# A two-block transformer kernel: the context's first modulation, norm and projections taken one k-tile at a time

## The chip, the cores and the metric

The kernel runs on one core of a Trainium2 chip. The metric is the device time of one execution in microseconds (us). Before the change three runs took 3097.56 to 3098.76 us, median 3098.48 us; one further execution was recorded by the hardware profiler, and every row below is from that one.

## The reference, cut to what matters

Two transformer blocks follow each other. The first has two layers and two streams: a latent stream of 512 tokens and a context stream of 256 tokens, both 1024 wide. Each layer starts with a modulated norm and one wide projection of each stream:

```python
mod = (jax.nn.silu(c) @ w_mod[l] + b_mod[l])[:, None, :]
mod_c = jax.nn.silu(c_ctx) @ w_mod[l] + b_mod[l]
sh1, sc1, ga1, sh2, sc2, ga2 = jnp.split(mod, 6, axis=-1)
sh1c, sc1c, ga1c, sh2c, sc2c, ga2c = jnp.split(mod_c, 6, axis=-1)
h = modulate(rmsnorm(x, g_norm1[l]), sh1, sc1)
hc = modulate(rmsnorm(xc, g_norm1[l]), sh1c, sc1c)
pf, mq, mk, mv, mo, mg, cq, ckv, kr = split_proj(h @ w_in[l])
pfc, mqc, mkc, mvc, moc, mgc, cqc, ckvc, krc = split_proj(hc @ w_in[l])
...
def modulate(h, shift, scale):
    return h * (1 + scale) + shift
```

So before the first projection of the context can run, its shift and scale (two of the six parts of `silu(c_ctx) @ w_mod[0]`) and its norm must be there. The rest of the program (Fourier mixing, an mLSTM, attention, MLPs, and the second block) is the same before and after.

## The kernel before

The feature dimension is cut into eight k-tiles of 128. A product in full precision is made of three passes over weights and activations that are split into a high and a low part: `gemm` (lines 194 to 196) issues `wh` times high, `wh` times low and `wl` times high for each k-tile. A weight unit comes through `wunit` (lines 158 to 177): a DMA on the SP queue into `wr`, a cast on ACT to `wh` (line 169), a subtraction on DVE to `wl` (line 170), in rings of three. A scheduler orders the instructions of each engine by priorities that the program sets; each engine then runs its own list strictly in that order.

The start of the program, layer 0:

- `mod_cols` makes `cs`, the two conditioning vectors through silu, as a column of two for each k-tile.
- `mod_first` makes the shift and scale of both streams. For each of four groups of 512 columns it loads eight weight tiles of 256 KB from `wmn` (SP queue), multiplies each with the two columns of `cs` (line 476, result 2x512), copies the row out on ACT (line 479), turns it by four transposes (line 483) and adds the bias on DVE (line 487). The two groups of the scale come first, then the two of the shift.
- `rms_bcast` (lines 251 to 274) makes one over the root mean square of each token: sums on TensorE (line 251), a power on POOL (line 222), a broadcast on TensorE (line 270), a copy on ACT (line 274, the tile `rb`).
- `mod_start` makes `cb`, the conditioning vectors on all partitions, for the modulations that DVE makes later (`mod_units`, line 442, done beside other work through a side queue): four broadcast DMAs of `cc`, then DVE and ACT work (lines 418 to 421).
- `norm_split` makes the normed, modulated activations of the context, each k-tile as high and low part: a multiply on DVE (line 285), a cast with bias on ACT (line 289), a subtraction on DVE (line 290).
- `in_tok` (lines 543 to 545) makes the token-major projections in 48 matmuls, 128x432 each; `in_qk` makes six feature-major units of 24 matmuls, 128x256 each, and their convolutions on DVE (lines 580 and 586).
- Then the latent stream's norm (same lines, 512 wide), and units that both streams share (24 matmuls of 256 columns for the context, 24 of 512 for the latents). The mLSTM gates of the context are added on DVE (line 642) and transposed on TensorE (lines 645 and 671).

The order of work around the change is thus: all of shift and scale, then the whole norm, then all products of `in_tok`, then the six units of `in_qk`.

## Time and profile before

| | before |
|---|---|
| median of 3 runs | 3098.48 us (3097.56 to 3098.76) |
| the profiled execution | 3100.99 us |
| its span on the core | 3099.2 us |
| TensorE (PE) busy | 3005.6 us, 97% of the span |
| VectorE (DVE) busy | 1869.3 us, 60% |
| ScalarE (ACT) busy | 1182.9 us, 38% |
| GpSimd (POOL) busy | 116.7 us, 4% |
| mean DMA rate over the span | 118 GB/s |
| mean granted TensorE clock | 0.984 |

The span is the time between the first and the last instruction of the core; the execution's own time lies 1.8 us above it. A clock of 1.00 is full speed (2.4 GHz), 0.50 the lower level (1.2 GHz). Times in the rows below count from the span's start.

### The profile page before, as it was taken

Reading aid. Unit: us, or ns where it says so; the run is one execution under the profiler, and the core shown is the slowest. Engines: PE = TensorE matmul, PEld = TensorE weight load, DVE = VectorE, ACT = ScalarE, POOL = GpSimd, SP = SyncE. Lnnn points to the kernel's source line nnn. Section 1 sums busy time; section 2 is a strip of 40 time slices with the busy share of each in tenths; the row PEclk is TensorE's granted clock in tenths of the full one; section 3 lists DMA queues with packets and bytes.
Section 4 is the critical chain, followed back from the end, with each engine's and each line's share of the span. In section 5 each row is a group of like instructions: output and inputs, shape, how many; then the busy total and the mean of one; then the engine's idle time right before and its main releaser. Section 6 shows DMA issues by size and latency. Waiting matters only on the chain.

```text
span 3099.2 us, 44553 instructions
## 1 busy us (share of the span) xinstructions
PE 3005.6 (97%) x17374; PEld 2557.9 (83%) x17374; DVE 1869.3 (60%) x3755; ACT 1182.9 (38%) x2101; POOL 116.7 (4%) x296
## 2 busy tenths in 40 slices
PE   8998899999999999999999999999999999999998
PEld 4788879788888877778888888999999878888886
DVE  5887756777655766543444666655555566655544
ACT  4455554353333455433334442322222442322223
POOL 1000000000000010000000100000000110000000
PEclk9999999999999999999999999999999999999999
DMA  8654535754555432122222312322222212322221
GB/s 307 200 181 143 152 94 180 240 177 161 170 169 168 141 119 84 38 82 96 95 95 91 109 42 76 100 84 94 89 89 92 100 49 76 109 92 96 95 95 68
DMA packets 138129, 367.14 MB, mean 118 GB/s; under 512 B 14864, under 2 KB 42960, under 8 KB 137920
## 3 DMA queue, kind: packets, MB, share of 16 engines
q1 hardware_dynamic: 135760, 361.59, 36.0%
q8 instruction: 137, 2.24, 0.3%
q10 hardware_dynamic: 1728, 2.24, 0.2%
q14 instruction: 72, 0.59, 0.1%
q0 software_dynamic: 432, 0.48, 0.1%
HBM read 349.09 MB, written 15.06 MB: 117 GB/s over the span
## 4 chain that ended last, share of the span: by engine, by line
PE 43%; issue 12%; DVE 1%; POOL 0%; ACT 0%; POOLq 0%; DVEq 0%; ACTq 0%
PE S L194 11%; PE S L196 11%; PE S L195 11%; PE D L1616 1%; PE S L1547 1%; PE S L1549 1%; PE S L1548 1%; PE S L1702 1%; PE D L1717 1%; PE S L1641 1%; PE S L1662 1%; PE D L1622 0%; PE S L1658 0%; PE D L1715 0%; PE D L1547 0%
## 5 line engine op out<-in xcount | busy, mean ns | idle before, releaser
L194 PE MATMUL S<-A,wh 128*128 128x512 f32 (+2 forms) x4416 | 1498.0, 340 | 12.8 <-ACT A L289 4.0
L196 PE MATMUL S<-A,wl 128*128 128x512 f32 (+2 forms) x4416 | 1492.4, 338 | 5.6 <-DVE wl L170 5.6
L195 PE MATMUL S<-A,wh 128*128 128x512 f32 (+2 forms) x4416 | 1493.2, 338 | 1.5 <-DVE A L185 1.4
L169 ACT CAST wh<-wr 128x1024 fp32r<-128x1024 f32 (+1 forms) x474 | 495.2, 1045 | 1380.0 <-PE S L195 862.0
L194 PEld LDWEIGHTS S<-A,wh 128*128 128x128 f32 x4416 | 835.7, 189 | 111.2 <-issue 6.1
L196 PEld LDWEIGHTS S<-A,wl 128*128 128x128 f32 x4416 | 835.8, 189 | 98.6 <-DVE wl L170 8.9
L195 PEld LDWEIGHTS S<-A,wh 128*128 128x128 f32 x4416 | 835.2, 189 | 94.9 <-DVE A L185 2.7
L170 DVE TENSOR_TENSOR wl<-wr,wh 128x1024 fp32r<-128x1024 f32 (+1 forms) x474 | 576.7, 1217 | 318.3 <-ACT wh L169 303.4
L442 DVE SCALAR_TENSOR_TENSOR wr<-wr,B 128x512 f32<-128x512 f32 x224 | 149.1, 686 | 73.1 <-DMA wr<-wmod 72.4
L212 DVE SCALAR_TENSOR_TENSOR A<-S,mod,A 128x512 f32<-128x512 f32 x144 | 107.7, 749 | 115.8 <-PE S L196 115.5
L210 DVE TENSOR_TENSOR A<-A,S 128x264 f32<-128x264 f32 (+1 forms) x168 | 85.3, 514 | 122.4 <-PE S L196 122.1
L185 DVE TENSOR_TENSOR A<-A,A 128x512 fp32r<-128x512 f32 (+3 forms) x168 | 102.3, 616 | 33.1 <-ACT A L184 32.8
L1869 DVE TENSOR_TENSOR A<-S,A 128x264 f32<-128x264 f32 (+1 forms) x66 | 34.3, 519 | 127.1 <-PE S L196 124.2
L184 ACT CAST A<-A 128x512 fp32r<-128x512 f32 (+3 forms) x168 | 93.1, 560 | 25.2 <-DVE A L1834 16.8
L1877 DVE SCALAR_TENSOR_TENSOR A<-A,S 128x264 f32<-128x264 f32 (+1 forms) x66 | 34.0, 515 | 86.7 <-PE S L196 84.4
L1024 PEld LDWEIGHTS S<-B,B 128*128 128x128 f32 x416 | 53.5, 194 | 16.5 <-issue 5.5
L1024 PE MATMUL S<-B,B 128*128 128x96 f32 x416 | 55.3, 276 | 4.5 <-ACT A L1029 2.3
L222 POOL TENSOR_TENSOR rnr<-rnv,mhalf 128x4 f32<-128x4 f32 (+1 forms) x19 | 23.5, 1238 | 951.7 <-DVE rnv L221 946.4
L580 DVE SCALAR_TENSOR_TENSOR A<-A,cw,A 128x512 f32<-128x512 f32 (+1 forms) x84 | 53.3, 635 | 2.6 <-ACT A L578 1.0
L996 PE MATMUL D<-A,A 96*128 96x256 f32 (+1 forms) x144 | 54.4, 482 | 0.0
L1079 ACT ACTIVATE A<-A 128x512 f32<-128x512 f32 x80 | 50.6, 632 | 2.2
L229 ACT ACTIVATE A<-A 128x512 f32<-128x512 f32 (+1 forms) x66 | 33.5, 535 | 45.8 <-DVE A L212 34.2
(410 smaller groups left out, 2872.2 us busy)
## 6 DMA issues: line engine op xcount, KB each, us to landing
wr<-wmod SPq DMA_DIRECT2D x112, 512.0 KB, 3.9
wr<-wup SPq DMA_DIRECT2D x96, 512.0 KB, 3.3
wr<-wdn SPq DMA_DIRECT2D x96, 512.0 KB, 3.5
wr<-win SPq DMA_DIRECT2D x78, 512.0 KB, 3.6
wr<-wg SPq DMA_DIRECT2D x44, 512.0 KB, 3.5
wr<-wu SPq DMA_DIRECT2D x44, 512.0 KB, 3.4
wr<-wd SPq DMA_DIRECT2D x44, 512.0 KB, 3.3
wr<-wout SPq DMA_DIRECT2D x40, 512.0 KB, 3.4
```

The lines of the kernel that those rows point to most:

```text
L169: nc.scalar.copy(hi, raw)
L170: nc.vector.tensor_sub(lo, raw, hi.bitcast(F32))
L184: self.nc.scalar.copy(hi, src)
L185: self.nc.vector.tensor_sub(lo, src, hi.bitcast(F32))
L194: nc.tensor.matmul(o, wh[:, k_w[i]], xh[:, ts], start=(i == 0), stop=False)
L195: nc.tensor.matmul(o, wh[:, k_w[i]], xl[:, ts], start=False, stop=False)
L196: nc.tensor.matmul(o, wl[:, k_w[i]], xh[:, ts], start=False, stop=(i == nk - 1))
L210: nc.vector.tensor_add(x[:, ts], x[:, ts], ps)
L212: nc.vector.scalar_tensor_tensor(out=x[:, ts], in0=ps, scalar=ga, in1=x[:, ts], op0=ALU.mult, op1=ALU.add)
L442: nc.vector.scalar_tensor_tensor(out=wf if i == len(which) - 1 else self.junk, in0=wf, scalar=1.0, in1=self.cb[s * 2 + hf], op0=ALU.mult, ...
L996: nc.tensor.matmul(sc[:, off : off + nk], qT[h][:, ts], kT[h], start=True, stop=True)
L1024: nc.tensor.matmul(yp, pT[:, kt], V[j][:, h * MD : h * MD + MD], start=(kt == 0), stop=(kt == tot // P - 1))
```

## The change

The modulations of shift and scale, the norm and most of the first products of the context now go k-tile by k-tile, in a new function `ctx_start`. For each of the eight k-tiles:

- four DMAs of 256 KB from `wmk` bring the 256 columns (scale and shift of this k-tile) of all eight input tiles;
- eight matmuls, each with 32 stationary columns of `cs` (two real, thirty zero) and 256 moving columns, write to one of four groups of 32 PSUM partitions, so that four partial sums stand under each other;
- ACT copies the 128x256 result out; two matmuls with the constant `sel` add the four groups and turn the result at once; DVE adds the biases (both streams) and makes the gain;
- `norm_split` runs for this k-tile alone;
- twelve matmuls of 128x256 add this k-tile's share to four of the six `in_qk` units (weights `wqk`, 256 KB a k-tile), and after every second k-tile twelve matmuls of 128x432 add to the `in_tok` results.

After the loop the four results are copied out, and `in_qk` has two units left. `mod_start` now makes `cb` by sixteen broadcast matmuls 128x128 and four ACT copies, with no DMA and no tanh of its own, and stands ahead of `rms_bcast`. The slots for modulation weights fall from 20 to 16.

```diff
@@ mod_start
+                ps = self.S.new([P, 512])
+                for k in range(4):
+                    nc.tensor.matmul(
+                        ps[:, k * P : k * P + P], self.cs[:, hf * 4 + k, s : s + 1].broadcast_to([P, P]), self.ident,
+                        start=True, stop=True,
+                    )
                 t = self.B.new([P, 512])
-                nc.sync.dma_start(out=t, in_=self.a["cc"][s, hf].partition_broadcast(P))
-                nc.vector.tensor_scalar_mul(t, t, 0.5)
-                nc.scalar.activation(self.junk, t, AF.Tanh)
-                nc.vector.scalar_tensor_tensor(out=t, in0=self.junk, scalar=1.0, in1=t, op0=ALU.add, op1=ALU.mult)
+                nc.scalar.copy(t, ps)
...
@@ mod_cols
+        wide = self.sm([P, KT, 32], "cs", bufs=1)
+        nc.gpsimd.memset(wide, 0.0)
...
+        nc.vector.scalar_tensor_tensor(out=wide[:, :, 0:2], in0=th, scalar=1.0, in1=cs, op0=ALU.add, op1=ALU.mult)
+        self.cs = wide
+        self.sel = self.sm([P, 2], "sel", bufs=1)
+        nc.scalar.dma_start(out=self.sel, in_=self.a["sel"])
+
+    def ctx_start(self, mr, nr, tr, xc, rb, mods, gn, hc):
...
+        sc, sh = part(mods[1], 1), part(mods[1], 0)
+        qk = [self.S.new([P, NX]) for _ in range(4)]
+        dm = self.pd.new([P, 2, 512])
+        dt = self.pd.new([P, 2, 512])
+        for k in range(KT):
+            ps = dm[:, 0, k % 2 * 256 : k % 2 * 256 + 256]
+            for q in range(KT):
+                if q % 2 == 0:
+                    w = mr.new([P, 2, 256])
+                    nc.sync.dma_start(out=w, in_=self.a["wmk"][k, q // 2])
+                g = q % 4 * 32
+                nc.tensor.matmul(ps[g : g + 32], self.cs[:, q], w[:, q % 2], start=(q < 4), stop=(q >= 4))
+                if q % 2:
+                    mr.drop(w)
+            row = nr.new([P, 256])
+            nc.scalar.copy(row, ps)
+            dd = dm[:, 1, k * 4 : k * 4 + 4].rearrange("p (i s) -> p i s", i=2)
+            for i in range(2):
+                nc.tensor.matmul(dd[:, i], row[:, i * P : i * P + P], self.sel, start=True, stop=True)
+            nr.drop(row)
+            cols = slice(k, k + KT + 1, KT)
+            for s in (1, 0):
+                nc.vector.tensor_add(mods[s][:, cols], dd[:, :, s], self.bmod[:, 0, cols])
+            kk = slice(k, k + 1)
+            nc.vector.scalar_tensor_tensor(
+                out=Ac[:, kk], in0=sc[:, kk], scalar=1.0, in1=gn[:, 0, 0, kk], op0=ALU.add, op1=ALU.mult
+            )
+            self.norm_split(nr, rb, hc, xc, NX, Ac, sh, [k])
+            hh, hl = hc[k]
+            wh, wl = self.wunit(self.a["wqk"][k])
+            for j, o in enumerate(qk):
+                cs = slice(j * P, j * P + P)
+                nc.tensor.matmul(o, wh[:, cs], hh, start=(k == 0), stop=False)
+                nc.tensor.matmul(o, wh[:, cs], hl, start=False, stop=False)
+                nc.tensor.matmul(o, wl[:, cs], hh, start=False, stop=(k == KT - 1))
+            if k % 2:
+                self.tok_products([dt[:, 0, 0:432], dt[:, 1, 0:432]], 0, hc, k // 2)
...
@@ the layer loop
+                else:
+                    steps, convs, qkc = self.in_qk(tr, pg, l, hc, NX, range(6), raws)
+                    call(steps[4:])
```

The order of TensorE's instructions, first place: the program's start, where the context's first product stands. In these rows `cs` is the conditioning tile, `A` names SBUF work tiles, `S` and `D` PSUM tiles, and the last entry is the shape of the result. Before:

```order
L476 MATMUL D_27_117<-A_35_139,cs_23_102 2x512
L251 MATMUL S_46_173<-ones_70,A_38_151 128x1
...
L270 MATMUL S_50_183<-ident_69,rnr_49_180 128x128
L476 MATMUL D_51_187<-A_52_188,cs_23_102 2x512
...
L476 MATMUL D_73_255<-A_81_277,cs_23_102 2x512
L543 MATMUL S_107_353<-wh_110_356,A_91_313 128x432
```

And now:

```order
L491 MATMUL D_64_199<-A_69_213,cs_23_102 32x256 x2
L415 MATMUL S_30_122<-ident_69,cs_23_102 128x128 x4
...
L247 MATMUL S_46_172<-ones_70,A_38_150 128x1
...
L498 MATMUL D_64_199<-sel_26_110,A_70_217 128x2 x2
L266 MATMUL S_50_182<-ident_69,rnr_49_179 128x128 x2
L491 MATMUL D_64_199<-A_75_246,cs_23_102 32x256 x2
...
L498 MATMUL D_64_199<-sel_26_110,A_79_262 128x2 x2
L512 MATMUL S_60_195<-A_51_186,wh_73_229 128x256
```

Before, all 32 column products (line 476) stand ahead of the first product of the context (line 543). Now those of two k-tiles do, and the sixteen broadcasts (line 415) stand ahead of the sums of the norm (line 247, line 251 of before).

Second place: TensorE where the latents' norm is made (rms sums, then broadcast, then the first shared units, where `wh_219` of before and `wh_233` of the change are the same weights). Before:

```order
L251 MATMUL S_191_720<-ones_70,A_190_718 128x1
L194 MATMUL S_223_805<-A_91_313,wh_219_795 128x256
L270 MATMUL S_195_734<-ident_69,rnr_194_731 128x128 x4
L195 MATMUL S_223_805<-A_91_313,wh_219_795 128x256
...
L194 MATMUL S_224_832<-A_167_682,wh_219_795 128x512
L194 MATMUL S_232_883<-A_91_313,wh_228_870 128x256
...
L645 MATMUL S_341_1706<-ident_69,A_340_1700 36x128
```

And now:

```order
L247 MATMUL S_205_803<-ones_70,A_204_801 128x1
L266 MATMUL S_209_817<-ident_69,rnr_208_814 128x128 x4
L190 MATMUL S_237_888<-A_51_186,wh_233_878 128x256
L191 MATMUL S_237_888<-A_51_186,wh_233_878 128x256
L190 MATMUL S_238_915<-A_181_765,wh_233_878 128x512
L191 MATMUL S_238_915<-A_182_766,wh_233_878 128x512
L695 MATMUL S_355_1789<-ident_69,A_354_1783 36x128
L721 MATMUL S_361_1808<-ident_69,A_354_1783 36x128
```

Before, two context units and most of a latent unit (70 matmuls) stand between the broadcast and the first gate transpose (line 645). Now four matmuls do (line 695 is line 645 of before), and the other 44 of the first shared unit come behind the transposes.

Third place: DVE from that norm's start to the gates' last addition. Before:

```order
L170 TENSOR_TENSOR wl_220_796<-wr_218_794,wh_219_795 128x1024
L442 SCALAR_TENSOR_TENSOR wr_222_801,macc_221_800<-wr_222_801,B_87_300 128x512
L221 TENSOR_SCALAR rnv_193_730<-S_191_720 128x4
L442 SCALAR_TENSOR_TENSOR wr_222_801,macc_221_800<-wr_222_801,B_88_305 128x512
L580 SCALAR_TENSOR_TENSOR A_242_1011<-A_147_565,cw_436,A_242_1011 128x256 x3
L170 TENSOR_TENSOR wl_229_871<-wr_227_869,wh_228_870 128x1024
L285 SCALAR_TENSOR_TENSOR A_197_741<-A_7_86,A_0_166_680,A_192_729 128x512
```

And now:

```order
L630 SCALAR_TENSOR_TENSOR A_248_1020<-A_151_637,cw_659,A_248_1020 128x256 x3
L217 TENSOR_SCALAR rnv_207_813<-S_205_803 128x4
L630 SCALAR_TENSOR_TENSOR A_248_1020<-A_151_637,cw_659,A_248_1020 128x256
L636 SCALAR_TENSOR_TENSOR A_249_1026<-A_249_1026,A_248_1020 128x256
L281 SCALAR_TENSOR_TENSOR A_211_824<-A_7_86,A_0_180_763,A_206_812 128x512
...
L692 TENSOR_TENSOR A_354_1783<-gk_0_155_651,bg_657 128x2x4
L166 TENSOR_TENSOR wl_234_879<-wr_232_877,wh_233_878 128x1024
```

Before, the subtractions for two shared units (`wl_220`, `wl_229`), seven convolution steps more and two modulation products were done ahead of the norm. Now they follow behind it (line 166 is line 170 of before, 630 is 580, 281 is 285, 692 is 642).

From about 230 us of the trace on (some 950 TensorE instructions into the list), the order of all engines is the same in both kernels.

## Rows read from the trace of the kernel before

**Rows 1.** Busy us of each engine by stretch (count), TensorE's granted clock, DMA share, GB/s.

```profile
20.00:30.00 10.00, 9.34 (x21) 1.72 (x19) 0.19 (x2) 0.57 (x1) 0.00 (x0) 0.78 1.05 388
79.00:91.00 12.00, 11.51 (x71) 9.58 (x70) 11.08 (x21) 7.81 (x13) 0.49 (x5) 1.00 0.12 44
91.00:106.30 15.30, 14.61 (x76) 12.17 (x75) 14.94 (x40) 10.32 (x17) 0.62 (x2) 1.00 0.80 254
```

**Rows 2.** The timeline of PE, 0 to 56 us: start, us, instruction, idle before.

```profile
15.14 1.02 PE L251 MATMUL S<-ones,A 128*128 128x1 f32 x8
...
29.37 0.41 PE L483 MATMUL D<-ident,A 2*128 2x2 f32 x4 [0.67 <-ACT A L479]
29.70 7.03 PE L476 MATMUL D<-A,cs 128*2 128x512 f32 x16
...
44.69 0.46 PE L543 MATMUL S<-wh,A 128*128 128x432 f32 x1
...
55.12 0.38 PE L194 MATMUL S<-A,wh 128*128 128x256 f32 x1
```

**Rows 3.** Groups by line and shape, 0 to 110 us: busy, mean ns, idle before.

```profile
L476 PE MATMUL D<-A,cs 128*2 128x512 f32 x64 | 32.7, 662 | 6.1 <-DVE cs L464 4.4 <-DMA A<-wmn 1.7
...
L289 ACT ACTIVATE A<-A,mod 128x256 fp32r<-128x256 f32 x8 | 3.5, 497 | 0.2 <-DVE mod L487 0.2
...
L285 DVE SCALAR_TENSOR_TENSOR A<-A,Ac,A 128x256 f32<-128x256 f32 x8 | 3.3, 480 | 0.1
...
L487 DVE TENSOR_TENSOR mod<-D,bmod 128x4 f32<-128x4 f32 x8 | 0.9, 156 | 15.1 <-PE D L483 15.1
```

**Rows 4.** The timeline of ACT, 0 to 32 us, and the DMA issues of 0 to 40 us.

```profile
8.56 0.33 ACTq L1132 DMA_DIRECT2D ident<-ident  x1
...
19.12 0.37 ACT L274 COPY A<-S 128x256 f32<-128x256 f32 x1 [3.44 <-PE S L270]
...
ident<-ident ACTq DMA_DIRECT2D x1, 64.0 KB, 5.2
```

**Rows 5.** The timeline of PE, 1805.9 to 1810 us: matmuls of 128 and of 64 columns.

```profile
1806.02 1.04 PE L1641 MATMUL S<-ident,B 128*128 128x128 f32 x8
1806.81 0.37 PE L196 MATMUL S<-A,wl 128*128 128x264 f32 x1
...
1808.54 1.04 PE L1662 MATMUL S<-B,A 128*64 128x128 f32 x16
1809.51 0.39 PE L194 MATMUL S<-A,wh 128*128 128x264 f32 x1
```

**Rows 6.** The timeline of PE, 71.9 to 107 us.

```profile
72.33 1.84 PE L251 MATMUL S<-ones,A 128*128 128x1 f32 x16
...
91.10 0.27 PE L671 MATMUL S<-ident,A 128*36 128x128 f32 x1
...
105.90 0.40 PE L196 MATMUL S<-A,wl 128*128 128x512 f32 x1
106.14 0.28 PE L194 MATMUL S<-A,wh 128*128 128x256 f32 x1
```

**Rows 7.** The timeline of DVE, 72 to 95 us.

```profile
76.33 1.22 DVE L170 TENSOR_TENSOR wl<-wr,wh 128x1024 fp32r<-128x1024 f32 x1
78.63 2.08 DVE L285 SCALAR_TENSOR_TENSOR A<-A,A,A 128x512 f32<-128x512 f32 x3 [1.07 <-ACT A L274]
...
90.47 0.16 DVE L642 TENSOR_TENSOR A<-gk,bg 128x8 f32<-128x8 f32 x1
```

**Rows 8.** What PE waited for, 106.3 to 230 us: us in total, times, longest.

```profile
PE S L740 <- DVE A L719: 2.7, 1, 2.7
PE S L855 <- DVE A L852: 1.7, 1, 1.7
```

**Rows 9.** As rows 1, two stretches at the lower clock.

```profile
17.60:24.40 6.80, 6.80 (x15) 1.85 (x14) 0.23 (x2) 0.37 (x1) 0.00 (x0) 0.50 1.05 393
75.60:79.00 3.40, 3.10 (x14) 3.10 (x15) 2.29 (x4) 0.90 (x2) 0.24 (x1) 0.50 0.69 204
```

More of the change, by code (lines that the diff above doesn't have):

```diff
@@ L50 @@
 NRR = 8
-MS = 4
 R4 = 0.8
@@ L463, in mod_cols @@
         nc.scalar.activation(th, cs, AF.Tanh)
-        nc.vector.scalar_tensor_tensor(out=cs, in0=th, scalar=1.0, in1=cs, op0=ALU.add, op1=ALU.mult)
-        self.cs = cs
-    def mod_first(self, ring, mods, cols):
-        nc = self.nc
-        cs = self.cs
-        for c in cols:
-            ps = self.pd.new([P, 512])
-            for k in range(KT):
-                w = ring.new([P, 512])
-                nc.sync.dma_start(out=w, in_=self.a["wmn"][k, MOD_PE.index(c)])
-                nc.tensor.matmul(ps[0:2], cs[:, k], w, start=(k == 0), stop=(k == KT - 1))
-                ring.drop(w)
-            row = ring.new([2, 512])
-            nc.scalar.copy(row, ps[0:2])
-            self.pd.drop(ps)
-            dd = self.pd.new([P, 4, 2])
-            for j in range(4):
-                nc.tensor.transpose(dd[:, j], row[:, j * P : j * P + P], self.ident[0:2, 0:2])
-            ring.drop(row)
-            cs_ = slice(c * 4, c * 4 + 4)
-            for s in range(2):
-                nc.vector.tensor_add(mods[s][:, cs_], dd[:, :, s], self.bmod[:, 0, cs_])
-            self.pd.drop(dd)
+        nc.vector.scalar_tensor_tensor(out=wide[:, :, 0:2], in0=th, scalar=1.0, in1=cs, op0=ALU.add, op1=ALU.mult)
@@ new lines, in mod_cols @@
+        self.cs = wide
+        self.sel = self.sm([P, 2], "sel", bufs=1)
+        nc.scalar.dma_start(out=self.sel, in_=self.a["sel"])
+    def ctx_start(self, mr, nr, tr, xc, rb, mods, gn, hc):
+        nc = self.nc
+        part = lambda m, i: m[:, i * KT : i * KT + KT]
+        Ac = self.sm([P, KT], "Ac")
+        sc, sh = part(mods[1], 1), part(mods[1], 0)
[35 more added lines that the diff above has]
+                self.tok_products([dt[:, 0, 0:432], dt[:, 1, 0:432]], 0, hc, k // 2)
+        nr.drop(rb)
+        raws = []
+        for o in qk:
+            raw = tr.new([P, NX + 4])
+            nc.gpsimd.memset(raw[:, 0:2], 0.0)
+            nc.gpsimd.memset(raw[:, NX + 2 : NX + 4], 0.0)
+            nc.scalar.copy(raw[:, 2 : NX + 2], o)
+            raws.append(raw)
+        out = self.tok_out([dt[:, 0, 0:432], dt[:, 1, 0:432]], NX, self.B)
+        self.S.drop(*qk)
+        self.pd.drop(dm, dt)
+        return out, raws
@@ L535, in in_tok, with tok_products, tok_out @@
                 feed((u * 2, u * 2 + 1))
[L536 to L545 removed]
+            self.tok_products(acc, l, h, u)
+        out = self.tok_out(acc, n, vr)
+        pg.drop(*held)
+        if nt == 4:
+            dr.drop(dd)
+        return out
+    def tok_products(self, acc, l, h, u):
+        nc = self.nc
+        wh, wl = self.wunit(self.a["wtok"][l, u])
+        for t, o in enumerate(acc):
+            ts = slice(t * P, t * P + P)
+            for k2 in range(2):
+                k = u * 2 + k2
+                cs = slice(k2 * 432, k2 * 432 + 432)
+                hh, hl = h[k]
+                nc.tensor.matmul(o, hh[:, ts], wh[:, cs], start=(k == 0), stop=False)
+                nc.tensor.matmul(o, hh[:, ts], wl[:, cs], start=False, stop=False)
+                nc.tensor.matmul(o, hl[:, ts], wh[:, cs], start=False, stop=(k == KT - 1))
+    def tok_out(self, acc, n, vr):
+        nc = self.nc
+        nt = n // P
         vt = [vr.new([P, 2, MH, 97]) for _ in range(nt // 2)]
@@ L564, in in_qk @@
         cw = self.cw[l]
-        raws = {}
+        raws = dict(enumerate(done or ()))
         def product(j):
@@ L1229, in block1 @@
                         nc.sync.dma_start(out=X[k], in_=a["xT"][:, k])
-                steps, convs, qkc = self.in_qk(tr, pg, l, hc, NX, range(6) if not last else range(3, 6))
-                call(steps)
                 if last:
+                    steps, convs, qkc = self.in_qk(tr, pg, l, hc, NX, range(3, 6))
+                    call(steps)
                     call(convs)
+                else:
+                    steps, convs, qkc = self.in_qk(tr, pg, l, hc, NX, range(6), raws)
+                    call(steps[4:])
                 self.wuq = self.turned(self.bcst, [P, 2, 512], F32, "wuq", 1)
@@ L2008, in _tables @@
     t["ident"] = np.eye(P, dtype=np.float32)
+    t["sel"] = np.eye(32)[:, :2].repeat(4, 0).reshape(32, 4, 2).transpose(1, 0, 2).reshape(P, 2)
     j = np.arange(64)
```

54 lines of the change are left out of this document (19 added, 35 removed).

## The prediction, made before the changed kernel ran

> **What bounds the kernel now.** I first read the busy time by engine: TensorE works 97% of the span, so a change at the start can only win or lose idle time and TensorE work there, and what it wins is carried to the end unless a later wait takes it back. The order of all engines is the same from about 230 us on, so the whole effect is decided before that, and I walk TensorE through that stretch in both orders.
>
> Next I read the stretches of the start. From 20 to 30 us TensorE is busy while DMA moves 388 GB/s, and its granted clock is 0.78 in the mean [rows 1]. In the norm of the latents, 79 to 91 us, TensorE is busy 11.51 of 12 us and DVE 11.08; up to 106.3 us DVE is busy 14.94 of 15.3 [rows 1]. So the first 45 us are TensorE with DMA, and the 30 us from the latents' norm on are DVE and TensorE side by side, both full.
>
> Then the timeline of TensorE. Eight column products, 16 instructions, take 7.03 us at full clock: 0.44 us for 512 columns, so 0.22 for 256. The 48 token-major products stand between 44.69 and 55.12 with four transposes: 10.43 / 52 = 0.20 us each [rows 2]. The six units of 24 follow until 72.33: 17.2 / 144 = 0.12 us each [rows 2, 6]. The reader is to see that nothing of the 45 us before 44.69 is product work on the context, and that the products then run without gaps.
>
> **What is removed.** All 64 instructions of the column products, 32.7 us of TensorE as they ran [rows 3], and their 256 KB loads; the same bytes come again in another cut. Of the loads of `cc` four go; the queue had them behind the last columns, where nobody waited, so I set them at nothing, as the DVE and ACT work that made `cb`.
>
> **What is added, first part: until the first product of the context.** The sixteen broadcasts need `ident`, which is issued at 8.56 us and takes 5.2 us: 13.8 us [rows 4]. The queue ahead of it is as full as before, so I keep that. The columns of the first k-tile are done before. A broadcast is two instructions of 128 columns; eight such take 0.79 us from 1806.02 to 1806.81 [rows 5], 0.10 each, so 32 take 3.2 us at full clock and 6.4 at half. The engine has just been idle for some microseconds, and the trace has a half-clock stretch of 6.8 us near there [rows 9]; I take the middle, 4.8, ending at 18.6. Behind it stand the sums of the norm. Before, they started at 15.14 [rows 2] and `rb` was ready at 19.12 + 0.37 = 19.5 [rows 4], 4.4 us later; now 23.0. Then the multiply 0.48, the cast 0.50 [rows 3] and some 0.5 us of handovers: first product at **24.5 us**, with 20.7 as the early end (broadcasts hidden, sums at 15.14 as before).
>
> **Second part: a pair of k-tiles.** Products: 24 x 0.12 + 12 x 0.20 = 5.3 us, as before, only moved. Columns: sixteen matmuls of two instructions, 0.22 us each if they run one after another, 7.0 us. No row shows four tiles of 32 columns. The nearest is the pair of 64-column tiles in the second block: 16 instructions take 0.97 us (1808.54 to 1809.51) where full-width ones at 0.10 would take 1.6 [rows 5]. That is half price, 0.79, and 0.18 left over for going back to full width. I read it so that the second instruction of one matmul runs beside the first of the next, which lies in another tile; the two of one matmul can't, and in the new order they stand in sequence as well. So four tiles give me the same two at a time: 32 x 0.11 = 3.5 us and three returns to full width, 4.0 us. The ends are 1.8 (four at a time) and 7.0.
>
> The page "TensorE: Matmul & The Clock Gate" of the Trainium skill, Part 3, has three column tiles start some 4 ns apart and gain 2.38 times. By it four tiles would go at nearly a quarter of the price, and the sum below would be about 3 us less; the row on the 64-column pair bears out that tiles overlap, and no row here shows more than two.
>
> Summing with `sel`: eight instructions that load 128 new stationary columns each, as the norm's sums, which take 1.02 us for eight with their tail [rows 2]; 0.9. Waits: before, TensorE stood 0.67 us for each row copy of 512 [rows 2]; now the copy is of 256, some 0.4, twice a pair. Behind it two additions at 0.16, the gain, multiply 0.48, cast 0.50 [rows 3] and handovers make 1.8 us; the columns of the next k-tile (1.9) hide the first chain, about 1.5 us of products the second. I take 1.1 us a pair in all, between 0 and 2.5. A pair is 5.3 + 4.0 + 0.9 + 1.1 = **11.3 us**.
>
> DMA does not bound it: the context, columns and weights are about 13 MB, some 35 us at 388 GB/s [rows 1], and though the SP queue stands once (the third `wqk` load waits for the subtraction that frees its buffer, at some 22 us), all is in before 45 us.
>
> The first pair has its columns done, so the products end at 24.5 + 5.3 + 3 x 11.3 = **63.7 us**. Before, the same work (`in_tok` and four units) was done at 55.12 + 96 x 0.12 = 66.6. With two units more, 5.7 us, the latents' sums start at 69.4 instead of 72.33 [rows 6]: **2.9 us won**.
>
> **Third part: the latents' norm.** From those sums to the norm's first multiply it is 78.63 - 72.33 = 6.3 us [rows 6, 7], and to the gates' last addition 11.8 more (90.47) [rows 7]: now 75.7 and 87.5, the transposes at 88.1. Before, TensorE had 70 matmuls for this time and was busy 11.51 of 12 us [rows 1]. Now four stand there, and then the transposes, which wait for DVE; what is queued behind them has its operands and must wait too. So some 11 us of idle time arise, and the work comes later: 44 matmuls (22 x 0.12 + 22 x 0.23) and two whole units (24 x 0.12 + 24 x 0.23 each), 24.8 us, until 112.9. The 0.23 is a 512-column step (105.90 to 106.14), and 106.14 is where the third shared unit ended before [rows 6]: **6.8 us behind**.
>
> DVE has put off two subtractions of 1.22 us [rows 7], seven convolution steps and two modulation products, 7.3 us (a convolution step as the 256-wide multiply, 0.48, a product 0.7), and started 2.9 earlier: 4.4 us behind. Later TensorE waits 2.7 and 1.7 us for DVE [rows 8]; with DVE 2.4 us less behind, these shrink by 2.4. That leaves 4.4. After an idle time of 11 us I expect the clock to fall, as it did after the 1.02 us wait at 75.6 us: 3.4 us at half [rows 9], 1.7 lost. Sum: **6.1 us slower**.
>
> The profiled execution took 3100.99 us, which is 2.5 above the median. 3100.99 + 6.1 - 2.5 = 3104.6; I say **3105 us**, a fifth of a per cent slower, and 0.2% (6.2 us) is about what a measurement of this kernel can tell from no change.
>
> **The rivals.**
> - *All small terms are on the good side* (the other sign). It turns on the start and the chain: if the broadcasts hide in the wait for the sums (first product at 20.7, 3.8 us), the tiles go four at a time and the chains hide (3.0 and 3.3 us), the norm starts at 65 us, no fall of the clock follows (1.7) and DVE's two waits vanish whole (2.0): 3104.6 - 13.8 = 3091 us. It wins from the point where a pair takes less than some 9 us and the first product stands by 22 us. For it: the 64-column pair; against it: the single queue of ACT, where casts, row copies and the norm's casts share one order.
> - *Half of that*: an early start or the overlap of four, not both, and shorter waits: 3.8 to 6.8 us less, 3098 us, no change.
> - *The tiles run one after another.* Then a pair costs 3.5 more less the 0.7 that they cover, 8.4 us, and the second k-tile's columns delay the first product by 1.8: 3115 us. Against it: the row of the 64-column pair.
> - *Each return to full width costs a whole pipeline.* Instead of 0.18 us, the tail of an instruction, 0.27 [rows 6], both ways, six times a pair: 1.6 less 0.5, times three, 3 to 4 us: 3108 us. The page "TensorEngine Tiling (Array Packing)" of the Trainium skill, Key Properties, says that a change of tiling mode drains the engine, which speaks against interleaving tiles and full-width products; the 0.18 us is all that the rows here show of it.
>
> **How the numbers follow.** Forecast 0.38 (3105, its own range 3100 to 3109), good side 0.26, half 0.18, one after another 0.08, whole pipeline 0.10. Faster by over 0.2% (under 3092.3): the good side and a little, 0.27. Slower (over 3104.7): the last two and about 0.24 of the forecast, 0.42. Within: 0.31. The range goes from 3089, below the good side's time, to 3113: it leaves out the serial case and the best of the good side, together 2 in 10.
>
> **What would show it.** Right: line 491 in steps of about 0.11 us an instruction; the first line 512 at about 24.5 us and the last at about 63; an idle stretch of some 11 us before line 695, ended by DVE at line 692; the third shared unit ending near 113; shorter waits for DVE behind it. Wrong: steps of 0.06 or 0.22; a first product by 21 us; no wait at line 695; or a difference that arises behind 230 us, where nothing is moved.

## The result and the profile after

The changed kernel takes **3118.18 us** (median of 5 runs, 3111.46 to 3123.38) where the kernel before takes 3098.76 (5 runs, 3097.56 to 3103.27): a ratio of **1.006, 95% interval 1.0042 to 1.0079**. Run again beside other kernels it took 3121.42 us, 1.0076 (1.0056 to 1.0096). The forecast was 3105 us, with a range to 3113. The change is slower, as forecast, but by 19 to 23 us instead of 6.

The profiled execution took 3111.46 us, the fastest of its five runs: 10.5 us more than the profiled one before (3100.99). I follow the forecast's walk in it first. TensorE's timeline from 12 to 24.4 us (start, us, instruction, idle before it):

```profile
14.37 5.17 PE L415 MATMUL S<-ident,cs 128*128 128x128 f32 x32 [3.61 <-DMA ident<-ident]
19.38 0.95 PE L247 MATMUL S<-ones,A 128*128 128x1 f32 x8
...
22.11 1.07 PE L491 MATMUL D<-A,cs 128*32 128x256 f32 x16
23.75 0.61 PE L498 MATMUL D<-sel,A 128*128 128x2 f32 x4 [0.57 <-ACT A L495]
24.22 0.37 PE L512 MATMUL S<-A,wh 128*128 128x256 f32 x1
```

The broadcasts wait for `ident` as said, and the first product starts at 24.22 us (forecast 24.5). The same view of later stretches answers to [rows 6]:

```profile
63.12 0.36 PE L594 MATMUL D<-wh,A 128*128 128x432 f32 x1
63.32 0.28 PE L190 MATMUL S<-A,wh 128*128 128x256 f32 x1
...
69.02 1.84 PE L247 MATMUL S<-ones,A 128*128 128x1 f32 x16
72.41 2.08 PE L266 MATMUL S<-ident,rnr 128*128 128x128 f32 x8 [1.55 <-POOL rnr L218]
78.30 0.58 PE L190 MATMUL S<-A,wh 128*128 128x256 f32 x1 [3.81 <-ACT wh L165]
...
85.55 0.37 PE L695 MATMUL S<-ident,A 128*36 128x128 f32 x1 [5.60 <-DVE A L692]
...
114.26 0.28 PE L190 MATMUL S<-A,wh 128*128 128x256 f32 x1
```

The context's products end at 63.3 us, the latents' sums start at 69.02 where they started at 72.33, and the third shared unit ends at 114.26 where it ended at 106.14: 8.1 us behind. So the 3 us won turn into 8 lost between 69 and 114 us, and the three bracketed stops, 1.55, 3.81 and 5.60 us, are where. What TensorE waited for behind that, 114.3 to 240 us (us, times, longest), answers to [rows 8]:

```profile
PE S L790 <- DVE A L769: 4.1, 1, 4.1
PE S L854 <- ACT A L930: 3.5, 2, 3.1
PE S L882 <- ACT A L876: 1.5, 1, 1.5
```

These are longer than before, not shorter: 9.1 us where [rows 8] has 4.4. Last, the busy time by stretch (PE, PEld, DVE, ACT, POOL; TensorE's clock; DMA share; GB/s), first before, then after:

```profile
24.00:60.00 36.00, 34.53 (x144) 18.08 (x143) 23.83 (x48) 20.50 (x35) 0.00 (x0) 0.99 0.85 303
60.00:90.00 30.00, 28.14 (x202) 26.27 (x200) 24.60 (x46) 16.68 (x30) 1.88 (x6) 0.94 0.60 206
120.00:165.00 45.00, 42.49 (x286) 37.27 (x285) 37.40 (x113) 19.01 (x58) 1.22 (x2) 1.00 0.72 225
```

```profile
24.00:60.00 36.00, 30.86 (x250) 23.10 (x249) 19.23 (x51) 15.86 (x31) 0.61 (x11) 1.00 1.00 348
60.00:90.00 30.00, 18.38 (x113) 15.91 (x112) 23.47 (x46) 18.72 (x33) 1.71 (x6) 0.70 0.37 128
120.00:165.00 45.00, 36.71 (x212) 31.03 (x213) 32.65 (x107) 16.23 (x51) 1.78 (x5) 0.89 0.57 176
```

From 60 to 90 us TensorE is busy 18.38 us where it was 28.14, while DVE is nearly as busy as before: the latents' norm needs the same time on DVE, and the context's projections that used to stand beside it on TensorE are already done. Take as a mark the first product of a token-major unit from which both kernels have the same 16,274 matmul instructions left (the common product). Before reaches it at 226.7 us, the change at 242.9, 16.2 us later. Summed over TensorE's rows up to there, the change computes 193.4 us at the full clock where before has 202.7 (9 us saved), but stands still for 39.7 us instead of 17.4, and loses 9.8 us to the lower clock instead of 6.7. The change saves work as it should, and pays for it more than twice over in waiting. At the end of the two profiled executions 10.5 of the 16.2 us are left, although the order behind the common product is the same: behind 240 us, before's profiled execution ran at half clock for 90 us, the change's for 64. The pair of profiles thus flatters the change, and the medians are the better measure of it. The experiments ask why it loses.

### The profile page after: what moved, and what is told of

Read it like the earlier page. It is cut to its first block, busy times and chain, and to the rows that moved or that the text cites. A ratio compares the mean times of both kernels' runs of the same rounds, so it can differ in the third digit from the quotient of the medians.

```text
span 3109.7 us, 44803 instructions
## 1 busy us (share of the span) xinstructions
PE 2995.1 (96%) x17486; PEld 2557.0 (82%) x17486; DVE 1867.6 (60%) x3766; ACT 1183.6 (38%) x2109; POOL 116.5 (4%) x297
## 4 chain that ended last, share of the span: by engine, by line
PE 43%; issue 12%; DVE 1%; POOL 0%; ACT 0%; POOLq 0%; DVEq 0%; ACTq 0%
PE S L190 11%; PE S L191 11%; PE S L192 11%; PE D L1669 1%; PE S L1600 1%; PE S L1602 1%; PE S L1601 1%; PE S L1755 1%; PE D L1770 1%; PE S L1694 1%; PE S L1715 1%; PE D L1675 0%; PE S L1711 0%; PE D L1768 0%; PE D L1600 0%
## 5 line engine op out<-in xcount | busy, mean ns | idle before, releaser
L165 ACT CAST wh<-wr 128x1024 fp32r<-128x1024 f32 (+2 forms) x478 | 495.9, 1037 | 1390.5 <-PE S L191 866.5
L192 PEld LDWEIGHTS S<-A,wl 128*128 128x128 f32 x4384 | 829.8, 189 | 101.9 <-DVE wl L166 10.6
L166 DVE TENSOR_TENSOR wl<-wr,wh 128x1024 fp32r<-128x1024 f32 (+2 forms) x478 | 577.5, 1208 | 336.0 <-ACT wh L165 323.9
```

Source lines behind the costliest of these rows:

```text
L165: nc.scalar.copy(hi, raw)
L166: nc.vector.tensor_sub(lo, raw, hi.bitcast(F32))
L192: nc.tensor.matmul(o, wl[:, k_w[i]], xh[:, ts], start=False, stop=(i == nk - 1))
```

## Experiments

**The order of the change, piece by piece.** Three kernels put one piece of the new order back, and a fourth (cols4) takes one piece of the change alone. qk_last moves the context's last two projections behind the latents' norm:

```diff
-                    call(steps[4:])
 ...
                     feed(range(KT))
+                    call(steps[4:])
```

> The changed kernel with only the last two feature-major context units issued behind the latents' norm, so that TensorE has 48 matmuls (5.7 us) between the norm's broadcast and the gate transposes. Theory A (blocked norm: the idle time of 5.6 + 3.8 + 1.6 us before line 695 is on the path): the idle time before line 695 falls by about 5.7 us, the third shared unit ends 5 to 6 us earlier than 114.3 us, the time is 5 to 10 us shorter than the changed kernel's, 3105 to 3114 us. Theory B (the loss lies in the pairs of k-tiles, before 63 us, which this leaves as they are): no shorter than the changed kernel by more than 2 us.

Measured: 3117.86 us, 1.0061 (1.0046 to 1.0077), no gain. The stop ahead of the gates goes, but the third shared unit ends at 115 us, no earlier, as 7.7 us of waiting for a weight's cast (ACT, `wh`) and 2.0 us for `wl` stand in its place: 5.7 us of TensorE's work, moved, cover nothing in the sum.

bcast_late moves the sixteen broadcasts of the modulations' input behind the context loop:

```diff
-        self.mod_start(jr)
 ...
         first, raws = self.ctx_start(mr, nr, tr, XC, rbc, mods[0], gn, hc)
+        self.mod_start(jr)
```

> The changed kernel with only the sixteen broadcast matmuls of the conditioning vectors moved behind the context's products. In this order the scheduler also puts one whole context unit and most of a latent unit ahead of the gate transposes again. Theory A (blocked norm): the idle time before line 695 is gone, the third shared unit ends near 105 us instead of 114.3, the time falls to 3098 to 3104 us. Theory B (only the late start counts): the first product stands at about 20.5 instead of 24.2 us and the whole is 4 us shorter than the changed kernel, 3107 to 3119 us.

Measured: 3109.16 us, 1.0038 (1.0024 to 1.0053): 9 us of the 20 come back in the medians. The first product starts no earlier (25.07 us), and no stop ahead of line 695 is left in its trace. But the trace does not show where the gain arises: the third shared unit ends at 116.2 us, not at 105, and the common product comes at 243.3 us, no earlier than in the change's profiled execution (242.9), the fastest of its five.

cols_first runs the columns of all eight k-tiles ahead of the first norm and product:

```diff
-        for k in range(KT):
+        def columns(k):
 ...
+        def products(k):
 ...
+        for k in range(KT):
+            columns(k)
+        for k in range(KT):
+            products(k)
```

> The changed kernel with the interleaving by k-tile undone: the columns of all eight k-tiles (still four column tiles) stand ahead of all norms and products; gate transposes behind 24 context and 17 latent matmuls. Theory A (the short chains of each k-tile, not the loads, keep TensorE waiting, and the four column tiles are what saves time): columns end near 30 us, products run without gaps to about 52 us instead of 63.3, and the time is 3088 to 3098 us. Theory B (interleaving is what hides the loads): products start only when 8 MB of columns are in and end no earlier than 62 us; 3105 us or more.

Measured: 3115.56 us, 1.0064 (1.0047 to 1.008). A k-tile's columns come every 2.6 us, 1.7 of which TensorE computes; the rest it waits for the copy and the additions. The columns end at 42 us, not near 30 as theory A has it. Interleaving is not what costs the 20 us.

cols4 is the kernel before with the column tiles alone, 512 columns wide, group by group, and nothing moved:

```diff
-                nc.tensor.matmul(ps[0:2], cs[:, k], w, start=(k == 0), stop=(k == KT - 1))
+                g = k % 4 * 32
+                nc.tensor.matmul(ps[g : g + 32], cs[:, k], w, start=(k < 4), stop=(k >= 4))
 ...
```

> The kernel before with one part of the change alone: its column products (512 columns, same loads, same order of work) write to four groups of 32 PSUM partitions, are summed with sel, and all else stays as before (conditioning vectors by DMA, whole norm, then whole products). Theory A (four column tiles are the gain of the change, the k-tile order and the broadcasts on TensorE its loss): columns are bound by their loads and end near 29 us, the first token-major product stands at 31 to 34 us instead of 44.7, the third shared unit ends 8 to 13 us before 106.1 us, and the time is 3084 to 3092 us. Theory B (what is won at the start is given back where DVE is full): the start is won as above, but the time lies within 4 us of before.

Measured: 3106.19 us, 1.0027 (1.0017 to 1.0038). The first token product starts at 39.09 us where it started at 44.69 [rows 2], and yet the kernel is 8 us slower. Its timeline and its waits up to 165 us:

```profile
39.09 0.87 PE L548 MATMUL S<-wh,A 128*128 128x432 f32 x2 [3.38 <-ACT wh L169]
...
54.09 0.39 PE L194 MATMUL S<-A,wh 128*128 128x256 f32 x1 [1.51 <-ACT wh L169]
...
73.83 1.84 PE L251 MATMUL S<-ones,A 128*128 128x1 f32 x16
```

```profile
PE S L745 <- DVE A L724: 5.4, 1, 5.4
PE S L548 <- ACT wh L169: 3.4, 1, 3.4
```

The 5.6 us won at 39 us are gone by the latents' sums: they start at 73.83 us, 1.5 us later than before (72.33 [rows 6]). In between TensorE waits for the casts and low parts of the first units' weights (0.83, 1.51 and 0.75 us), and its granted clock is 0.79 from 36 to 60 us where before has 1.00. The wait of 5.4 us for DVE ahead of the recurrence's transposes (line 745) comes on top. So less work for TensorE at the start is worth nothing by itself. one_group asks the reverse in the changed kernel, with every column product in the same 32 columns of the array:

```diff
-                g = q % 4 * 32
-                nc.tensor.matmul(ps[g : g + 32], self.cs[:, q], w[:, q % 2], start=(q < 4), stop=(q >= 4))
+                g = 0
+                nc.tensor.matmul(ps[g : g + 32], self.cs[:, q], w[:, q % 2], start=(q == 0), stop=(q == KT - 1))
 ...
```

> The changed kernel with all column products in one group of 32 PSUM partitions, so that none can run beside another. The changed kernel's 16 instructions of line 491 took 1.1 to 1.2 us. Theory A (four tiles run nearly four at a time): here they take 3.4 to 3.6 us (0.22 each) and a pair of k-tiles 3 to 5 us more. Theory B (the low price has another reason, such as the 256 columns or the 32 stationary columns): they take under 2 us here too.

One run: 3122.97 us, which lies within the change's own runs (3111 to 3131). Up to the common product, at 249.8 us, TensorE computes 213.5 us, 20 more than in the change, and waits 28.0 instead of 39.7. The four tiles save 20 us of TensorE's work and 7 us of the time up to there.

**DVE's load.** The modulations of the later parts are made on DVE in the stretch behind the norm. mods_later lets fewer of them in there and more later:

```diff
-RQ = [1.5, 2, 2]
+RQ = [0.5, 2.75, 2.5]
```

> The changed kernel with fewer of the later modulations (line 442 on DVE) during the shared units (rate 0.5 instead of 1.5 a unit, 2.75 and 2.5 instead of 2 and 2 afterwards). Theory A (the context's recurrence on DVE is late because put-off DVE work and modulations stand ahead of it): TensorE's wait for line 769 falls from 4.1 to 4.4 us to under 1.5 us and the time to 3106 to 3114 us. Theory B (the recurrence is late by its own chain): the wait stays above 3 us, and the time as the changed kernel's.

Measured: 3131.99 us, 1.0114 (1.0096 to 1.0131). The recurrence is through at 114.3 us instead of 123.1, and the wait for it falls to 1.8 us, but the modulations pile up behind it: TensorE then waits 7.1 us in one piece for DVE, ahead of a norm's sums (line 247). To take the load away without paying later, before_light and after_light shorten 32 of those dot products to 16 of 512 columns in either kernel, so that their results lack the rest:

```diff
-                    wf = w[:, hf * 512 : hf * 512 + 512]
+                    n = 16 if l == 0 and which == [1] else 512
+                    wf = w[:, hf * 512 : hf * 512 + n]
```

> The kernel before with the DVE products of layer 0's first 32 modulation units cut from 512 to 16 columns (it leaves out most of those dot products; loads stay), some 38 us of DVE work less in the first 300 us. It is the partner of after_light. Expected under both theories: TensorE's wait of 2.7 us for the context's recurrence shrinks or goes, the time falls by 3 to 15 us.

> The changed kernel with the same products cut from 512 to 16 columns (most of those dot products left out). Theory A (behind the norm the changed kernel loses time because DVE reaches the recurrence late): TensorE's wait for line 770 (769 of the changed kernel) falls from 4.1 to 4.4 us to under 1.5 us, and the gap to before_light is 5 to 12 us, what was lost by 114 us, where it is 20 us between the full kernels. Theory B (DVE's load has no part in it): the wait and a gap of 15 us or more stay.

Measured: 3099.97 us (1.0013, 1.0003 to 1.0022) and 3117.63 us (1.007, 1.0053 to 1.0088). The recurrence's last step but one starts 6.6 us earlier than in the change (116.09 us for 122.70), and the time does not move; before_light is no faster than before either, against the 3 to 15 us that both theories expected. The gap between the two kernels is still 17.7 us. The load of these modulations on DVE is not what costs. after_light's waits of 60 to 165 us show what stayed:

```profile
PE S L696 <- DVE A L693: 5.6, 1, 5.6
PE S L190 <- ACT wh L165: 3.8, 1, 3.8
PE S L791 <- DVE A L770: 3.2, 1, 3.2
```

The other direction, modulations earlier, in the room that cols4 leaves (`R1` 0.5 and 1.0 in place of 0):

> The kernel before with four column tiles (as cols4) and modulation units at a rate of 0.5 instead of 0 during the ten units of the context's first products, so that DVE does five of them (7 us) in time that it stood idle. Theory A (cols4 loses its head start because DVE is the bound up to the recurrence): the recurrence ends 4 to 7 us earlier than in cols4 (122.3 us), and the time falls from 3106 to 3094 to 3101 us. Theory B (the loads of the modulations crowd out those of the products): no faster than cols4.

> As cols4_r05 with a rate of 1.0, ten units (14 us of DVE). Theory A: the recurrence ends earlier still or as in cols4_r05. Theory B: the products' weights come late and the first third of the program gets longer than in cols4.

Measured: 3116.11 us (1.0063, 1.005 to 1.0077) and 3133.4 us (one run), both slower than cols4, so theory A fails. That the loads crowd out those of the products fits, but is not shown.

**The clock.** after_again, the changed kernel once more, shows how far its runs differ:

> The changed kernel once more, to see where its runs differ. The first five runs took 3111.5 to 3123.4 us, and the mean granted clock falls from 0.985 to 0.980 as they get longer. Theory A (the idle stretches that the change makes, above all the 11 us before the gate transposes, are followed by stretches at half clock of varying length): again 3111 to 3123 us, some 15 us longer where the mean clock is 0.005 lower, and if the profiled execution is a long one, its extra half-clock stretch lies in the first 250 us. Theory B (the spread comes from anywhere in the program): extra half-clock stretches lie behind 250 us, where nothing is moved.

3114.13 to 3130.63 us in 6 runs, median 3121.42. In its profiled execution TensorE also runs at half clock in the first columns:

```profile
23.37 1.81 PE L491 MATMUL D<-A,cs 128*32 128x256 f32 x16
25.73 1.01 PE L498 MATMUL D<-sel,A 128*128 128x2 f32 x4 [0.55 <-ACT A L495]
```

This execution (3123.59 us) is 12.1 us longer than the change's first profiled one, and the half-clock stretches in its trace make 117 us where that one has 94. Half of the difference is 11.4 us, nearly the whole 12.1. 10 of the 23 us lie before 240 us and 13 behind, where nothing is moved, so both theories have a part. What brings the stretches about from run to run is not shown.

The profiled execution of the change had 20.5 us at half clock that begin with the stops:

```profile
71.80:92.30 20.50, 9.89 (x39) 7.96 (x40) 17.54 (x35) 12.69 (x19) 1.05 (x6) 0.50 0.21 62
```

after_warm keeps TensorE at work in the two stops and leaves all else (28 and 20 calls):

```diff
+    def warm(self, h, cnt):
+        d = self.pd.new([P, 2, 512])
+        for i in range(cnt):
+            self.nc.tensor.matmul(d[:, 0, 0 : h.shape[-1]], h[:, 0:P], h, start=True, stop=True)
+        self.pd.drop(d)
```

> The change with 48 products added whose sums nobody reads: 28 of 256 columns (28 x 0.12 = 3.4 us at the full clock) behind the latents' sums, where TensorE stood still for 1.55 and 3.81 us, and 20 of 512 columns (20 x 0.235 = 4.7 us) ahead of the gates' transposes, where it stood still for 5.60 us. No step that anything waits for moves by more than a microsecond. Theory C (the slow clock that follows these stops is a good part of the loss): the half-clock stretch of 20.5 us from 71.8 us on is gone or short, PE's clock in 60 to 90 us is over 0.95 where it was 0.70, the third shared unit ends near 110 us where it ended at 114.3, and the time falls by 4 to 6 us, to 3112 to 3114. Theory I (the loss is waiting behind other engines, whatever the clock): the clock is full in that stretch too, but what TensorE wins there it waits again, ahead of the recurrence's transposes (over 6 us there, where it was 4.1) and behind; the time stays within 2 us of the change's, 3116 to 3120.

> The kernel before with the column tiles alone (3106.2, 1.0027) and the same added products: 28 ahead of the first token product, where it stood still for 3.4 us, 20 ahead of the gates' transposes. Theory C: the half-clock stretches from 39.4 and 56.4 us on (10.2 us together, 5 us of loss) go, and the time falls by 3 to 5 us to 3101 to 3103, still no better than before's 3096 to 3099. Theory I: it stays within 2 us of 3106.

Measured: 3117.67 us, 1.007 (1.0056 to 1.0083), and 3106.71 us, 1.0027 (1.0017 to 1.0037): the times without the added products. after_warm by stretch, and what it waited for from 60 us on:

```profile
60.00:90.00 30.00, 25.10 (x164) 21.79 (x163) 24.30 (x48) 19.23 (x35) 1.71 (x6) 0.94 0.38 135
90.00:120.00 30.00, 30.00 (x167) 26.44 (x167) 25.09 (x67) 13.46 (x25) 1.17 (x4) 0.95 0.77 235
```

```profile
PE S L798 <- DVE A L777: 5.5, 1, 5.5
PE S L862 <- ACT A L938: 2.9, 1, 2.9
PE S L703 <- DVE A L698: 2.7, 1, 2.7
```

The clock is 0.94 where it was 0.70, and the wait ahead of the recurrence's transposes grows from 4.1 to 5.5 us. The slow clock behind the stops is a symptom; TensorE has time there.

**The gates' place in the queues.** The stop of 5.60 us ends with DVE's line 692, the addition of the gates' bias. DVE's timeline there, and POOL's row that feeds it:

```profile
75.14 2.08 DVE L281 SCALAR_TENSOR_TENSOR A<-A,A,A 128x512 f32<-128x512 f32 x3 [2.73 <-ACT A L270]
...
84.42 0.74 DVE L286 SCALAR_TENSOR_TENSOR A<-A,mod,A 128x512 fp32r<-128x512 f32 x1
85.09 0.31 DVE L692 TENSOR_TENSOR A<-gk,bg 128x8 f32<-128x8 f32 x3
...
86.06 1.22 DVE L166 TENSOR_TENSOR wl<-wr,wh 128x1024 fp32r<-128x1024 f32 x1
```

```profile
83.29 0.22 POOL L687 MEMSET A<- 128x144 f32 x1 [10.94 <-DVE A L281]
```

The gates' columns were there at 66 us. Their additions of 0.16 us stand behind fifteen steps of the latents' norm on DVE; the tile that they fill takes a place that a step of that norm frees (POOL clears it at 83.29 us); and on TensorE their transposes stand ahead of nearly all of the first shared unit. after_gates gives that tile a place of its own and its first steps a rank ahead of the norm; before_gates does the same without the change:

```diff
+        early = l == 0 and n == NX
+        if early:
+            self.tc.cur_priority = 90000
-        gp = ring.new([P, nt, 2, R])
+        gp = self.sm([P, nt, 2, R], "gp", bufs=1) if early else ring.new([P, nt, 2, R])
 ...
```

> The change with the context's gates moved ahead: their tile has a place of its own (before, its clearing on POOL waited for a place that the latents' norm frees at 83.3 us), and their additions, transposes and forget gates stand ahead of the latents' norm in every queue. With that the first shared unit's low parts move ahead on DVE too, behind three of the eight latents' k-tiles. Theory G (the place of the gates in TensorE's queue, in front of the first shared unit, is what turned the saved work into a stop): the stop of 5.6 us ahead of the gates is gone and no other of over 3 us takes its place before 90 us; the third shared unit ends at 105 to 108 us where it ended at 114.3, the recurrence's transposes start 5 to 10 us earlier than 123.3, and the time falls by 6 to 10 us, to 3108 to 3112. Theory N (the latents' norm, 16 steps of 0.74 us on DVE from 75 us on, sets the pace there, and the gates only stood behind it): TensorE waits as long in front of the latents' products; the third unit ends no earlier than 111 us, and the time stays at 3115 to 3120.

> The same edit in the kernel before, where TensorE stood still for no microsecond ahead of the gates. Both theories: no stop is there to win; the 2.7 us ahead of the recurrence's transposes may go, so 3094 to 3099 where the kernel before has 3097 to 3099. If it gains as much as after_gates does, the order of the gates says nothing about the change.

Measured: **3108.57 us, 1.0039 (1.0022 to 1.0056)**, and 3099.53 us, 1.0008 (0.9996 to 1.002). The edit gives back 9.6 us of the changed kernel's 19.4 and nothing in the kernel before. after_gates on TensorE:

```profile
73.56 0.38 PE L727 MATMUL S<-ident,gp 128*36 128x128 f32 x2
...
79.50 0.58 PE L190 MATMUL S<-A,wh 128*128 128x256 f32 x1 [3.15 <-ACT wh L165]
...
80.95 0.57 PE L192 MATMUL S<-A,wl 128*128 128x256 f32 x1
...
108.69 0.28 PE L190 MATMUL S<-A,wh 128*128 128x256 f32 x1
```

The shared unit runs through from 79.50 us; in the change its fifth product, the first with `wl`, waited until 87.33. The third unit ends at 108.69 us: 5.6 us earlier than in the change, just past the 105 to 108 expected, with the recurrence's transposes 3.2 us earlier (120.08; 5 to 10 were expected). In this order the scheduling also put `wl` of the first shared unit ahead of most of the norm on DVE, so the gain belongs to both, the gates and that subtraction. The wait ahead of the recurrence's transposes stays (4.2 us). Before's trace has no such stop ahead of the gates, which fits that the same edit is worth nothing there.

**What is left.** late_gates joins after_gates and bcast_late (both diffs above), cols4_gates the gates and cols4:

> Both edits that shortened the change's idle time so far: the spreading of the columns' input behind the context loop (bcast_late, 3109.2) and the gates ahead (after_gates, 3108.6). If the two losses are separate (the gates' place in the queues, and the 8.8 us that TensorE idles more before 63 us), the gains add up to 3099 to 3102, level with the kernel before. If both edits win the same wait, it stays at 3106 to 3110.

> The column tiles alone with the gates ahead. In that kernel the context's products still stand in front of the gates, as in the kernel before, where the edit was worth nothing: 3104 to 3107. If the stop of 5.4 us ahead of its recurrence's transposes is due to the gates' place, it gains up to 5 us: 3100 to 3103.

Measured: 3108.62 us, 1.0031 (1.0019 to 1.0043), and 3109.52 us, 1.0036 (1.0024 to 1.0049). The two gains don't add. Whether bcast_late and after_gates win the same wait, as the expectation has it, the traces do not show: late_gates reaches the common product at 243.0 us, after_gates at 235.0. And where the context's projections still stand in front of the gates, as in cols4, the gates' place costs nothing. No version beats the kernel before; the 10 us between it and after_gates stay without a cause shown. In after_gates's trace TensorE still stands still for 32.5 us up to the common product (before: 17.4), 8 us of the difference before 64 us and the rest behind.

## Why the prediction was wrong

- **The start: right.** First product 24.22 us (24.5), last 63.3 (63.7), latents' sums 69.02 (69.4). Of the rivals for the start, neither the early one (20.7 us) nor the serial tiles happened.
- **A pair of k-tiles: nearly the right sum, wrong parts.** The trace has 10.6 and 10.9 us a pair (33.09 to 43.73 to 54.64 us) for 11.3. The columns were mis-sized, as this view of TensorE in the change shows, with two rows of one_group behind it:

```profile
26.41 0.62 PE L491 MATMUL D<-A,cs 128*32 128x256 f32 x2
26.96 0.51 PE L512 MATMUL S<-A,wh 128*128 128x256 f32 x2
...
33.09 1.07 PE L491 MATMUL D<-A,cs 128*32 128x256 f32 x16 [0.39 <-DVE mod L502]
34.29 0.75 PE L512 MATMUL S<-A,wh 128*128 128x256 f32 x4
...
36.95 1.05 PE L491 MATMUL D<-A,cs 128*32 128x256 f32 x10
37.93 0.74 PE L512 MATMUL S<-A,wh 128*128 128x256 f32 x4
...
41.34 0.63 PE L491 MATMUL D<-A,cs 128*32 128x256 f32 x6
42.73 0.61 PE L498 MATMUL D<-sel,A 128*128 128x2 f32 x4 [0.76 <-ACT A L495]
43.73 1.07 PE L491 MATMUL D<-A,cs 128*32 128x256 f32 x16 [0.39 <-DVE mod L502]
...
54.64 1.07 PE L491 MATMUL D<-A,cs 128*32 128x256 f32 x16 [0.39 <-DVE mod L502]
```

```profile
41.05 1.48 PE L491 MATMUL D<-A,cs 128*32 128x256 f32 x6 [0.39 <-DVE mod L502]
42.46 0.50 PE L512 MATMUL S<-A,wh 128*128 128x256 f32 x2
```

  From their start to that of the next row (less its idle time), blocks of 2 and 6 column instructions hold TensorE for 0.55 and 0.63 us, blocks of 10 and 16 for 0.98 and 1.07 to 1.20. In one_group six take 1.41. The single records of the trace say why: in the block at 33.09 us the first instructions of four products, each in its own tile, start within 0.03 us of each other, and the next four follow 0.22 us later. So a step of up to four tiles takes 0.22 us, as one instruction does in one_group; the two instructions of one product do run one behind the other, as I said, and 2 and 6 instructions make two steps, 10 and 16 four. What was wrong is that four tiles would stay at two at a time. Part 3 of the Trainium skill's page "TensorE: Matmul & The Clock Gate" has each tile of a set add some 4 ns to its span, which as an estimate makes four tiles nearly four times as fast. The trace agrees: starts 0.01 us apart. The return to full width is no dearer with four tiles than with one: the next product starts 0.31 us behind the last column instruction of a block, here and in one_group, and the products on either side of a block take some 0.1 us longer in both. The Trainium skill's page "TensorEngine Tiling (Array Packing)", Key Properties, says that a change of tiling mode drains the engine; these tenths are all that the traces show of it. In a pair the columns took 2.8 and 2.7 us instead of 4.0, the products beside them 5.8 instead of 5.3, the sums 0.9 as said, and the waits 1.2 and 1.6 instead of 1.1.
- **The new idle time: right.** "Some 11 us of idle time arise" ahead of line 695: 1.55 + 3.81 + 5.60 = 11.0 us, the last ended by line 692. The third shared unit was forecast 6.8 us behind and is 8.1 behind.
- **The step that failed: "these shrink by 2.4".** Behind the third unit TensorE's waits were to fall from 4.4 to 2.0 us, since DVE would be less far behind than TensorE. They rose to 9.1, and from the third unit to the common product the change goes from 8.1 to 16.2 us behind: 4.4 us of it are standing still, 3.2 the lower clock (in this account; after_warm shows that time at the lower clock can turn into standing still). DVE's delay was not far off: it reaches the recurrence's line 769 6.7 us later than before reaches line 719 (122.70 for 115.96 us), although the gates were 4.5 us earlier, because from the gates' last addition it runs 16 convolution steps, 6 low-part subtractions and 20 modulation products, where before ran 9, 4 and 15 (at 0.48, 1.22 and 0.69 us that is 9 us more; the forecast had 7.3), and waits 2.0 us for modulation weights. What I compared it with was wrong. TensorE is 8.1 us late at the third unit, but only 5.3 us late at the recurrence's transposes: from that unit to them it has 32 products in the new order where before had 44, and is busy for 4.90 us (114.26 to 123.30) where before was busy for 7.65 (106.14 to 116.50). With less work to cover it, the wait grew from 2.7 to 4.1 us, and 5.0 us of waiting for ACT (lines 930 and 876), which the forecast did not have, came behind it. after_light shows that the modulations' part of DVE's delay is no price by itself.
- **The clock: mis-sized, and of no weight.** 1.7 us were set for it. Half of the 9.89 busy us in the stretch above is 4.9, and after_warm, without it, is no faster.
- **From the profile to the median.** The forecast took 2.5 us off, as the profiled execution before lies above its median. The changed kernel's profiled execution lies 6.7 below its own. These 9.2 us and the 4.4 by which the profiled execution itself missed (10.5 against 6.1) are the 13.6 us from 3104.6 to 3118.2. The pair of profiles is luck in part: behind the common product, where the forecast had no difference, it comes from 16.2 to 10.5 us. The changed kernel's runs spread over 12 us and more with their time at half clock (after_again above); what sets that time is open, and after_warm, without the stops, spreads as wide (3111.65 to 3122.11).

What the walk lacked is a view of covers. The change moves the context's projections out of the stretch in which DVE makes the latents' norm and into one where TensorE waits for chains of small steps. I saw the new hole, and priced it as a delay that later slack gives back. Shown by after_gates is that about half of the loss hung on what stood in the hole: the gates ahead of the shared unit, and that unit's low part behind the norm. The other half is open.

## What to carry to other kernels

Work that an engine does beside another engine's long stretch is a cover; before moving it forward, ask what the engine will run in that stretch instead, and look at which short chain stands first in its queue there. Saved engine time is worth what the next wait leaves of it: here 9 us of TensorE's work saved came back as 22 us of waiting. A slow clock behind a stop may be the sign of a wait and not its price; adding work nobody needs tells the two apart cheaply.

## What the runs showed of the hardware that was not expected

Column products of 256 columns in four tiles of 32 columns run four at a time: their instructions start within 0.03 us of each other, and a step of four takes 0.22 us, as one instruction takes in one tile (one_group). The two instructions of one product run one behind the other, so a product alone gains nothing (0.55 us for its two), while eight products take 1.07 to 1.20 us. Blocks of tiles between full-width products cost little beyond their steps: the next product starts 0.31 us behind the last column instruction, with four tiles as with one. And 8 us of added products (after_warm) were free in time, as were the 10 us less at half clock that they brought.
